# Eight experts on one core: synchronisation by hand in one section in place of a scheduled kernel

## The chip, the core and the metric

The kernel runs on one core of a Trainium2 chip. The metric is the device time of one execution in microseconds (us), as the median of several runs. A profiler also records one execution: every instruction on the five engines (TensorE for matrix products, VectorE, ScalarE, GpSimd and SyncE) and every packet that the core's 16 DMA engines move between the off-chip memory (HBM) and the on-chip one (SBUF). Products are summed up in PSUM, a small memory that VectorE and ScalarE then read. Engines run by themselves; they wait for each other on semaphores, which are counters.

## The reference

Eight experts each apply a layer with a ReLU and a second layer to their own 256 rows. All arrays are float32.

```
n_experts, capacity, hidden, expert_hidden = 8, 256, 512, 2048
h = np.matmul(x, w1) + b1[:, np.newaxis, :]
h = np.maximum(h, 0)
return (np.matmul(h, w2) + b2[:, np.newaxis, :]).astype(np.float32)
```

Here w1 is 8 x 512 x 2048 and w2 is 8 x 2048 x 512: 4.19 MB per expert and array, 67 MB in all. x and the output have 4.19 MB each.

## The kernel before, in words

The kernel is written for a tile framework: buffers come from pools with a number of copies each, and the framework's scheduler puts in all semaphores. `ordered` keeps an instruction in its written order on its engine.

**Loads.** GpSimd's queue carries all weights, because its transfers convert float32 to float16 on the way (`load_w1`, L84; `load_w2`, L93); the wide loads of x for experts 2 to 3 and 4 to 7 go the same way (`load_x`, L76). x of experts 0 and 1 is loaded as float32 by SyncE (L194) and converted by VectorE (L203). There are three buffers for w1 and three for w2, so the load of expert e waits until TensorE has done with expert e - 3. The list `ring` holds the loads in order, each with the step from which it may be issued. Weights of the last two experts' w2 come in two halves (`HALVED`).

**Steps.** The main loop has steps s = 0 to 10. Step s runs the first product of expert s and the second product of expert s - 3 (`LAG`). TensorE therefore always has the first product of a later expert ahead of the second product of an earlier one; steps 8, 9 and 10 hold only the second products of experts 5, 6 and 7.

**First product** (L121): for each of 16 slices j, four matmuls of 256 columns make the transposed slice of h in a PSUM tile `ph` (three copies). ScalarE adds b1, applies the ReLU and writes `hT` (L128). The right-hand side `xT` comes from VectorE's transposes of 32 x 32 blocks (L109 and L112), which are written in the middle of the first product before.

**Second product** (L171 and L178): for each of the two blocks of 128 rows (tb 0 and 1) one matmul with a row of ones puts in b2, and 16 matmuls of 512 columns add up the slices in PSUM tiles `po`. There are two copies of the pair `po0`, `po1`. For the halved experts the order is: first half of the slices for tb 0 and tb 1, then the second half for both. For the others all 16 of tb 0 come first.

**Store**: VectorE copies `po0` (L156), ScalarE copies `po1` (L157). Results of experts 0 to 3 and of 4 and 5 are collected and written by GpSimd's queue at its end, behind all loads (`flush`, L140). Expert 6 is written in three parts, two by SyncE and one by ScalarE, and expert 7 by SyncE (L164). L252 is the program's own start, L263 its end.

Of the kernel before, what the change touches and what calls it, by code (L numbers as in the profile page):

```python
# [10 lines left out]
def kernel(  # L11
# [8 lines left out]
):  # L20
    nc = tc.nc
    fp32 = mybir.dt.float32
    fp16 = mybir.dt.float16
    E, T, H = x.shape
# [4 lines left out]
    nJ = M // P  # L29
    B = 32  # L30
    nB = P // B
    LAG = 3

    GROUPS = {0: 4, 4: 2}
    HALVED = (E - 2, E - 1)


    PARTS = {E - 2: ((0, 25, False), (25, 121, True), (121, 128, False))}  # L40
    nXF32 = 2
    X_LOADS = {2: 2, 4: 4}

    def ordered(ins):
        return tc.keep_in_program_order(ins)

    singles = ctx.enter_context(tc.tile_pool(name="singles", bufs=1))
    w1_pool = ctx.enter_context(tc.tile_pool(name="w1", bufs=3))
    w2_pool = ctx.enter_context(tc.tile_pool(name="w2", bufs=3))
    x_pool = ctx.enter_context(tc.tile_pool(name="xp", bufs=1))  # L50
    xT_pool = ctx.enter_context(tc.tile_pool(name="xTp", bufs=2))
    hT_pool = ctx.enter_context(tc.tile_pool(name="hT", bufs=LAG + 1))
    group_pool = ctx.enter_context(tc.tile_pool(name="groups", bufs=1))
    out_pool = ctx.enter_context(tc.tile_pool(name="outp", bufs=2))
# [3 lines left out]
    ones1 = singles.tile([1, P], fp16)  # L58
    b2_sb = singles.tile([1, E * H], fp16)
    b1_rows = singles.tile([E * nB, M // nB], fp32)  # L60
    b1T = singles.tile([P, nJ * B + nB - 1], fp32)

    x16 = [None] * E
    xT = [None] * E
    w1_sb = [None] * E
    w2_sb = [None] * E
    hT = [None] * E
    pending = {}
    results = {}
    group_of = {first + i: (first, n) for first, n in GROUPS.items() for i in range(n)}  # L70

    def load_x(first, n):

        R = n * T // P
        t = x_pool.tile([P, R, H], fp16, tag=f"x{first}", name=f"x{first}")
        ordered(nc.gpsimd.dma_start(  # L76
            out=t, in_=x[first : first + n].rearrange("e (p r) h -> (e p) r h", r=R)
        ))
        for i in range(n):
            x16[first + i] = (t, i * (P // n), R)  # L80

    def load_w1(e):
        w1_sb[e] = w1_pool.tile([P, nKC, M], fp16, tag="w1", name="w1sb")
        ordered(nc.gpsimd.dma_start(  # L84
            out=w1_sb[e], in_=w1[e].rearrange("(p kc) m -> p kc m", kc=nKC)
        ))

    def load_w2(e):
        src = w2[e].rearrange("(p j) h -> p j h", j=nJ)
        w2_sb[e] = w2_pool.tile([P, nJ, H], fp16, tag="w2", name="w2sb")  # L90
        half = nJ // 2 if e in HALVED else nJ
        for lo in range(0, nJ, half):
            ordered(nc.gpsimd.dma_start(out=w2_sb[e][:, lo : lo + half], in_=src[:, lo : lo + half]))  # L93

    def transposes(e):


        t, p0, R = x16[e]
        n = R // nTB
        xT[e] = xT_pool.tile([P, nKC, T], fp16, tag="xT", name="xT")  # L100
        for g in range(T // R // B):
            src = t[p0 + B * g : p0 + B * (g + 1)]
            for b in range(nB):
                block = src[:, :, b * (H // nB) : (b + 1) * (H // nB)].rearrange(
                    "p (n tb) (i kc) -> p tb kc n i", tb=nTB, kc=nKC)
                out = xT[e][b * B : (b + 1) * B].rearrange(
                    "p kc (tb g i n) -> p tb g kc n i", tb=nTB, i=B, n=n)
                if n == 1:
                    nc.vector.transpose(out=out[:, :, g, :, 0, :], in_=block[:, :, :, 0, :])  # L109
                    continue  # L110
                for tb in range(nTB):
                    nc.vector.transpose(out=out[:, tb, g], in_=block[:, tb])  # L112

    def first_product(e):
        hT[e] = hT_pool.tile([P, nJ, T], fp16, tag="hT", name="hT")
        split = group_of[e][1] if e in group_of else 1
        for j in range(nJ):
            bias_at = j * B + e * nB + nB - 1
            ph = psum_h.tile([P, T], fp32, tag="ph", name="ph")
            for kc in range(nKC):  # L120
                ordered(nc.tensor.matmul(  # L121
                    out=ph,
                    lhsT=w1_sb[e][:, kc, :].rearrange("p (q j) -> p q j", j=nJ)[:, :, j],
                    rhs=xT[e][:, kc, :],
                    start=(kc == 0),
                    stop=(kc == nKC - 1),
                ))
            nc.scalar.activation(  # L128
                out=hT[e][:, j, :].rearrange("p (tb k i) -> p tb k i", tb=nTB, k=split),
                in_=ph.rearrange("p (tb i k) -> p tb k i", tb=nTB, k=split),  # L130
                func=mybir.ActivationFunctionType.Relu,
                bias=b1T[:, bias_at : bias_at + 1],
                scale=1.0,
            )
            if j == nJ // 2 and e + 1 < E:
                transposes(e + 1)

    def flush(first):
        dst, src = pending.pop(first)
        ordered(nc.gpsimd.dma_start(out=dst, in_=src))  # L140

    def store(e, po):
        if e in group_of:
            first, n = group_of[e]
            split, rows = n, P // n
            if e == first:
                results[e] = group_pool.tile(
                    [P, split * nTB, H], fp32, tag=f"out{e}", name=f"out{e}")
        else:
            first, n, split, rows = e, 1, 1, P  # L150
            results[e] = out_pool.tile([P, nTB, H], fp32, tag="out", name="out")
        out_sb = results[first]
        at = (e - first) * rows
        for k in range(split):
            part = slice(k * rows, (k + 1) * rows)
            nc.vector.tensor_copy(out=out_sb[at : at + rows, k * nTB, :], in_=po[0][part])  # L156
            nc.scalar.copy(out=out_sb[at : at + rows, k * nTB + 1, :], in_=po[1][part])  # L157
        dst = out[first : first + n].rearrange("e (p r) h -> (e p) r h", r=split * nTB)
        if e in group_of:
            if e == first + n - 1:  # L160
                pending[first] = (dst, out_sb)
            return
        for p0, p1, scalar in PARTS.get(e, ((0, P, False),)):
            (nc.scalar if scalar else nc.sync).dma_start(out=dst[p0:p1], in_=out_sb[p0:p1])  # L164

    def second_product(e):
        po = []
        for tb in range(nTB):
            t = psum_o.tile([P, H], fp32, tag=f"po{tb}", name=f"po{tb}")
            po.append(t)  # L170
            ordered(nc.tensor.matmul(  # L171
                out=t, lhsT=ones1, rhs=b2_sb[0:1, e * H : (e + 1) * H], start=True, stop=False,
            ))
        half = nJ // 2 if e in HALVED else nJ
        for lo in range(0, nJ, half):
            for tb in range(nTB):
                for j in range(lo, lo + half):
                    ordered(nc.tensor.matmul(  # L178
                        out=po[tb],
                        lhsT=hT[e][:, j, tb * P : (tb + 1) * P],  # L180
                        rhs=w2_sb[e][:, j, :],
                        start=False,
                        stop=(j == nJ - 1),
                    ))
        store(e, po)

    warm = singles.tile([1, P], fp16)
    nc.vector.memset(ones1, 1.0)  # L188
    ordered(nc.scalar.activation(out=warm, in_=ones1, func=mybir.ActivationFunctionType.Relu))  # L189
    ordered(nc.scalar.dma_start(out=b1_rows, in_=b1.rearrange("e (b i) -> (e b) i", b=nB)))  # L190
    x32 = []
    for e in range(nXF32):
        x32.append(out_pool.tile([P, nTB, H], fp32, tag="out", name="x32"))
        nc.sync.dma_start(out=x32[e], in_=x[e].rearrange("(p tb) h -> p tb h", tb=nTB))  # L194
    load_w1(0)
    ordered(nc.gpsimd.dma_start(  # L196
        out=b2_sb,
        in_=b2.rearrange("e h -> (e h)").rearrange("(o f) -> o f", o=1),
    ))

    for e in range(nXF32):
# [3 lines left out]
        if e == 0:  # L205
            transposes(e)
# [22 lines left out]
    for s in range(E + LAG):  # L229
# [3 lines left out]
        if s < E:  # L233
            first_product(s)
# [33 lines left out]
```

## Time and profile before

| | |
|---|---|
| time, median of 3 runs | 181.53 us (181.39 to 182.13) |
| span of the profiled execution, first to last instruction | 179.7 us |
| median less span | 1.8 us |
| mean granted TensorE clock | 0.919 |
| transfers on GpSimd's queue | 38.28 MB, 96.4% of the 16 engines' time |

The profiled execution has no time of its own beside its span; 1.8 us is what the median of the runs has over it. A page of the profile gives the busy time of each engine, the span cut into 40 slices with one digit each (9 is 90% busy or more), the DMA queues, the chain of work that ended last, and groups of instructions by line. PE is TensorE, PEld its loading of the stationary operand, DVE is VectorE, ACT ScalarE, POOL GpSimd and SP SyncE; a q behind an engine means its instruction queue. In a row such as `158.43 1.17 ACT L157 COPY ... [10.26 <-PE po L178]` the numbers are the start and the length in us, and the bracket tells how long the engine had been idle and what ended that. In the waits view a row reads: who waited, for whom, us in total, times, longest. A group's row gives busy us, mean ns of one, and the idle time ahead of it with its cause.

### The profile page before, as it was taken

Reading aid. Unit: us, or ns where it says so; the run is one execution under the profiler, and the core shown is the slowest. Engines: PE = TensorE matmul, PEld = TensorE weight load, DVE = VectorE, ACT = ScalarE, POOL = GpSimd, SP = SyncE. Lnnn points to the kernel's source line nnn. Section 1 sums busy time; section 2 is a strip of 40 time slices with the busy share of each in tenths; the row PEclk is TensorE's granted clock in tenths of the full one; section 3 lists DMA queues with packets and bytes.
Section 4 is the critical chain, followed back from the end, with each engine's and each line's share of the span. In section 5 each row is a group of like instructions: output and inputs, shape, how many; then the busy total and the mean of one; then the engine's idle time right before and its main releaser. Section 6 shows DMA issues by size and latency. Waiting matters only on the chain.

```text
span 179.7 us, 1958 instructions
## 1 busy us (share of the span) xinstructions
PE 130.7 (73%) x784; PEld 87.4 (49%) x784; DVE 87.4 (49%) x125; ACT 71.0 (40%) x152; POOL 12.5 (7%) x27
## 2 busy tenths in 40 slices
PE   0005999159895970999769994959499986999960
PEld 0004899149793320794359543934189432434420
DVE  0999938990000199999998699203200020301010
ACT  3001699318793022491267406930559020020010
POOL 6000030200201010001100001000200021010000
PEclk9999999858999696599988999999969997899998
DMA  5999999999998999999999999999999999999995
GB/s 208 274 197 213 233 204 208 230 224 193 228 233 184 224 233 219 193 230 230 193 219 233 212 197 233 230 193 219 233 208 201 233 212 202 217 215 213 344 422 239
DMA packets 3844, 40.56 MB, mean 226 GB/s; under 512 B 460, under 2 KB 476, under 8 KB 1148
## 3 DMA queue, kind: packets, MB, share of 16 engines
q0 software_dynamic: 3200, 38.28, 96.4%
q1 hardware_dynamic: 476, 1.70, 2.5%
q10 hardware_dynamic: 160, 0.46, 0.6%
q8 instruction: 6, 0.10, 0.2%
q14 instruction: 2, 0.02, 0.0%
HBM read 71.39 MB, written 4.19 MB: 421 GB/s over the span
## 4 chain that ended last, share of the span: by engine, by line
DMA 67%; PE 27%; POOL 1%; issue 1%; ACT 0%; another core or an unknown queue 0%; POOLq 0%
DMA w1sb<-in_w_dram 44%; DMA w2sb<-in_w_dram 23%; PE po L178 17%; PE ph L121 10%; PE po L171 1%; POOL w1sb L84 1%; ACT out L157 0%; POOL b_sb L196 0%; POOL x L76 0%; POOLq L252 0%
## 5 line engine op out<-in xcount | busy, mean ns | idle before, releaser
L121 PE MATMUL ph<-xT,w1sb 128*128 128x256 f16 x512 | 66.7, 299 | 36.2 <-DMA w1sb<-in_w_dram 30.0
L121 PEld LDWEIGHTS <-w1sb 128*128 128x128 f16 x512 | 60.9, 148 | 42.7 <-DMA w1sb<-in_w_dram 38.6
L128 ACT ACTIVATE hT<-ph,b1T 128x256 f16<-128x256 f32 x128 | 56.7, 475 | 36.9 <-PE ph L121 22.1
L112 DVE STREAM_TRANSPOSE xT<-x 32x256 f16<-32x256 f16 (+1 forms) x64 | 52.7, 885 | 28.0 <-DMA x<-in_x_dram 22.0
L178 PE MATMUL po<-w2sb,hT 128*128 128x512 f16 x256 | 59.9, 395 | 6.6 <-DMA w2sb<-in_w_dram 6.5
L178 PEld LDWEIGHTS <-hT 128*128 128x128 f16 x256 | 25.7, 101 | 40.7 <-issue 14.4
L156 DVE COPY out<-po 32x512 f32<-32x512 f32 (+2 forms) x22 | 15.1, 688 | 52.5 <-PE po L178 52.2
L157 ACT COPY out<-po 32x512 f32<-32x512 f32 (+2 forms) x22 | 12.7, 578 | 65.5 <-PE po L178 65.3
L109 DVE STREAM_TRANSPOSE xT<-x 32x256 f16<-32x256 f16 x32 | 14.0, 436 | 0.5
L93 POOL DMA_DIRECT2D w2sb<-in_w_dram x10 | 5.3, 535 | 73.9 <-PE po L178 73.9
L84 POOL DMA_DIRECT2D w1sb<-in_w_dram x8 | 4.5, 559 | 62.7 <-PE ph L121 61.9
L171 PE MATMUL po<-b_sb,ones 1*128 1x512 f16 x16 | 4.8, 379 | 0.0
L210 DVE STREAM_TRANSPOSE b1T<-b_rows 32x512 f32<-32x512 f32 x4 | 4.1, 1028 | 0.0
L203 DVE CAST x<-x 128x1024 f16<-128x1024 f32 x2 | 1.4, 694 | 3.3 <-DMA x<-in_x_dram 3.3
L171 PEld LDWEIGHTS <-ones 1*128 1x128 f16 x16 | 0.9, 92 | 2.1 <-issue 2.1
L140 POOL DMA_DIRECT2D out_dram<-out x2 | 1.1, 540 | 11.1 <-ACT out L157 11.1
L189 ACT ACT_TABLE_LOAD x1 | 1.3, 1283 | 0.7 <-PEq L252 0.7
L76 POOL DMA_DIRECT2D x<-in_x_dram x2 | 1.1, 557 | 0.0
L188 DVE MEMSET ones<- 1x128 f16 x1 | 0.2, 165 | 0.8 <-PEq L252 0.8
L196 POOL DMA_DIRECT2D b_sb<-in_b_dram x1 | 0.5, 507 | 0.0
L189 ACT ACTIVATE warm<-ones 1x128 f16<-1x128 f16 x1 | 0.3, 308 | 0.0
L252 POOL MEMSET const-float32-0.0<- 128x1 f32 x1 | 0.1, 98 | 0.2 <-issue 0.2
(3 smaller groups left out, 0.3 us busy)
## 6 DMA issues: line engine op xcount, KB each, us to landing
w1sb<-in_w_dram POOLq DMA_DIRECT2D x8, 2048.0 KB, 37.0
w2sb<-in_w_dram POOLq DMA_DIRECT2D x6, 2048.0 KB, 49.7
w2sb<-in_w_dram POOLq DMA_DIRECT2D x4, 1024.0 KB, 24.0
out_dram<-out POOLq DMA_DIRECT2D x1, 2048.0 KB, 26.7
x<-in_x_dram SPq DMA_DIRECT2D x2, 512.0 KB, 4.0
x<-in_x_dram POOLq DMA_DIRECT2D x1, 1024.0 KB, 35.6
out_dram<-out POOLq DMA_DIRECT2D x1, 1024.0 KB, 17.7
x<-in_x_dram POOLq DMA_DIRECT2D x1, 512.0 KB, 24.5
```

The costliest lines, as they stand in the source:

```text
L84: ordered(nc.gpsimd.dma_start(out=w1_sb[e], in_=w1[e].rearrange("(p kc) m -> p kc m", kc=nKC)))
L93: ordered(nc.gpsimd.dma_start(out=w2_sb[e][:, lo : lo + half], in_=src[:, lo : lo + half]))
L109: nc.vector.transpose(out=out[:, :, g, :, 0, :], in_=block[:, :, :, 0, :])
L112: nc.vector.transpose(out=out[:, tb, g], in_=block[:, tb])
L121: ordered(nc.tensor.matmul(out=ph, lhsT=w1_sb[e][:, kc, :].rearrange("p (q j) -> p q j", j=nJ)[:, :, j], rhs=xT[e][:, kc, :], start=(kc == 0),
L128: nc.scalar.activation(out=hT[e][:, j, :].rearrange("p (tb k i) -> p tb k i", tb=nTB, k=split), in_=ph.rearrange("p (tb i k) -> p tb k i", ...
L156: nc.vector.tensor_copy(out=out_sb[at : at + rows, k * nTB, :], in_=po[0][part])
L157: nc.scalar.copy(out=out_sb[at : at + rows, k * nTB + 1, :], in_=po[1][part])
L171: ordered(nc.tensor.matmul(out=t, lhsT=ones1, rhs=b2_sb[0:1, e * H : (e + 1) * H], start=True, stop=False,))
L178: ordered(nc.tensor.matmul(out=po[tb], lhsT=hT[e][:, j, tb * P : (tb + 1) * P], rhs=w2_sb[e][:, j, :], start=False, stop=(j == nJ - 1),))
L189: ordered(nc.scalar.activation(out=warm, in_=ones1, func=mybir.ActivationFunctionType.Relu))
L210: nc.vector.transpose(out=b1T[b * B : (b + 1) * B, nB - 1 - b : nB - 1 - b + nJ * B], in_=b1_rows.rearrange("r (i j) -> r j i", j=nJ),)
```

## The change

The whole body is put into one section (`tc.tile_critical()`) that the scheduler treats as one piece. Within it every buffer is allocated by hand and every wait is written out on a semaphore of the kernel's own. Buffers keep their count (three of w1 and of w2, two of xT, four of hT), with these differences:

- `ph` has four PSUM buffers, not three; TensorE takes two credits at a time, one per buffer, and ScalarE gives one back with each activation.
- `po` has one pair, not two. TensorE takes `s_free[tb]` before it starts tb of the next expert; VectorE (tb 0) or ScalarE (tb 1) gives it after the copy.
- SyncE waits for each landing of weights and then counts up `s_go`; TensorE takes counts from that one semaphore and doesn't wait for a transfer itself.
- All experts' second products run in two halves of the slices, and the bias matmul of tb stands right ahead of the first half of tb.
- Every engine's program is written out one after the other: SyncE's stores of expert 6 stand between the two counts for expert 7's w2.
- At the section's end SyncE waits for all transfers of the output.

The order of the loads on GpSimd's queue, the sizes of all transfers and the number and shapes of the matmuls, activations, transposes and copies are unchanged. The core of the diff:

```diff
-    psum_h = ctx.enter_context(tc.tile_pool(name="psum_h", bufs=3, space=bass.MemoryType.PSUM))
-    psum_o = ctx.enter_context(tc.tile_pool(name="psum_o", bufs=2, space=bass.MemoryType.PSUM))
+    ctx.enter_context(tc.tile_critical())
+    ph = ctx.enter_context(nc.psum_tensor("ph", [P, NPH, H], fp32))
+    po = ctx.enter_context(nc.psum_tensor("po", [P, nTB, H], fp32))
+    def load(engine, key, **kw):
+        landed[key] = sem(f"d_{key}")
+        engine.dma_start(**kw).then_inc(landed[key], 16)
...
     def load_w1(e):
+        if e >= NW:
+            nc.gpsimd.wait_ge(s_ph, nJ * (e - NW + 1))
...
     def load_w2(e):
+        if e >= NW:
+            nc.gpsimd.wait_ge(s_po[1], e - NW + 1)
...
+    def flush(first):
+        n = GROUPS[first]
+        for tb in range(nTB):
+            nc.gpsimd.wait_ge(s_out[tb], first + n)
...
+    def evict(e, tb):
...
+        engine.wait_ge(s_po[tb], e + 1)
+        for k in range(n):
+            last = copy(out=results[e][at : at + rows, k * nTB + tb, :],
+                        in_=po[k * rows : (k + 1) * rows, tb, :])
+        last.then_inc(s_out[tb], 1)
+        if e + 1 < E:
+            engine.wait_ge(s_out[tb], e + 1)
+            engine.sem_inc(s_free[tb], 1)
...
+    def go(key, n=1):
+        nc.sync.wait_ge(landed[key], 16)
+        nc.sync.sem_inc(s_go, n)
     for s in range(E + LAG):
+        if s == 0:
+            nc.sync.wait_ge(landed["b2"], 16)
         if s < E:
+            go(f"w1_{s}")
+        e = s - LAG
+        if e >= 0 and e not in HALVED:
+            go(f"w2_{e}_0", 2)
+        elif e == E - 2:
+            go(f"w2_{e}_0")
+            go(f"w2_{e}_{half}")
+        elif e == E - 1:
+            go(f"w2_{e}_0")
+            for tb in range(nTB):
+                nc.sync.wait_ge(s_out[tb], e)
+            store(E - 2, 0, 25, nc.sync)
+            store(E - 2, 121, P, nc.sync)
+            go(f"w2_{e}_{half}")
+    for tb in range(nTB):
+        nc.sync.wait_ge(s_out[tb], E)
+    store(E - 1, 0, P, nc.sync)
...
+    def take(s, n=1):
+        nc.tensor.wait_ge(s, n).then_inc(s, -n)
+    for s in range(E + LAG):
+        nc.tensor.wait_ge(s_credit, NPH)
+        if s < E:
+            take(s_go)
+            take(s_xT)
+            for j in range(nJ):
+                if j % 2 == 0:
+                    take(s_credit, 2)
+                for kc in range(nKC):
+                    last = nc.tensor.matmul(
...
+                last.then_inc(s_ph, 1)
         if s >= LAG:
+            for lo in range(0, nJ, half):
+                take(s_go)
+                for tb in range(nTB):
+                    if lo == 0:
+                        take(s_free[tb])
+                        nc.tensor.matmul(po[:, tb, :], ones1[:], b2_sb[:, e * H : (e + 1) * H],
+                                         start=True, stop=False)
+                    for j in range(lo, lo + half):
+                        last = nc.tensor.matmul(
...
+                    if lo:
+                        last.then_inc(s_po[tb], 1)
+    for key, done in landed.items():
+        if key.startswith("out"):
+            nc.sync.wait_ge(done, 16)
```

More of the change, by code (lines that the diff above doesn't have):

```diff
@@ L23 @@
     fp16 = mybir.dt.float16
+    relu = mybir.ActivationFunctionType.Relu
     E, T, H = x.shape
@@ L29 @@
     nJ = M // P
+    half = nJ // 2
     B = 32
@@ L59 @@
[L59 to L68, printed above, removed]
-    results = {}
-    group_of = {first + i: (first, n) for first, n in GROUPS.items() for i in range(n)}
-    def load_x(first, n):
-        R = n * T // P
[L75 to L80, printed above, removed]
@@ L82, in load_w1, with sbuf, sem @@
-    def load_w1(e):
[L83 to L86, printed above, removed]
+    group_of = {first + i: (first, n) for first, n in GROUPS.items() for i in range(n)}
+    ctx.enter_context(tc.tile_critical())
+    def sbuf(name, shape, dtype):
+        return ctx.enter_context(nc.sbuf_tensor(name, shape, dtype))
+    def sem(name):
+        return ctx.enter_context(nc.semaphore(name=name))
@@ new lines @@
+    ones1 = sbuf("ones1", [1, P], fp16)
+    warm = sbuf("warm", [1, P], fp16)
+    b2_sb = sbuf("b2_sb", [1, E * H], fp16)
+    b1_rows = sbuf("b1_rows", [E * nB, M // nB], fp32)
+    b1T = sbuf("b1T", [P, nJ * B + nB - 1], fp32)
+    w1_sb = sbuf("w1_sb", [P, NW * nKC * M], fp16)
+    w2_sb = sbuf("w2_sb", [P, NW * nJ * H], fp16)
+    xT = sbuf("xT", [P, 2 * nKC * T], fp16)
+    hT = sbuf("hT", [P, (LAG + 1) * nJ * T], fp16)
+    x32 = [sbuf(f"x32_{e}", [P, nTB, H], fp32) for e in range(2)]
+    x16 = {}
@@ new lines @@
+    for e in range(2):
+        x16[e] = (sbuf(f"x_{e}", [P, nTB, H], fp16), 0, nTB)
+    x_group = {}
+    for first, n in X_LOADS.items():
+        R = n * T // P
+        x_group[first] = sbuf(f"x_{first}", [P, R, H], fp16)
+        for i in range(n):
+            x16[first + i] = (x_group[first], i * (P // n), R)
+    results = {}
+    for first, n in GROUPS.items():
+        t = sbuf(f"out_{first}", [P, n * nTB, H], fp32)
+        for i in range(n):
+            results[first + i] = t
+    results[E - 2], results[E - 1] = x32
@@ new lines @@
+    ph = ctx.enter_context(nc.psum_tensor("ph", [P, NPH, H], fp32))
+    po = ctx.enter_context(nc.psum_tensor("po", [P, nTB, H], fp32))
+    landed = {}
+    def load(engine, key, **kw):
+        landed[key] = sem(f"d_{key}")
+        engine.dma_start(**kw).then_inc(landed[key], 16)
+    s_ones = sem("ones")
+    s_self = sem("dve_self")
+    s_b1 = sem("b1T")
+    s_xT = sem("xT")
+    s_ph = sem("ph")
+    s_credit = sem("ph_free")
+    s_po = [sem(f"po{tb}") for tb in range(nTB)]
+    s_free = [sem(f"po{tb}_free") for tb in range(nTB)]
@@ new lines, with load_x @@
+    s_out = [sem(f"out{tb}") for tb in range(nTB)]
+    s_go = sem("weights")
+    for e in range(2):
+        load(nc.sync, f"x{e}", out=x32[e][:], in_=x[e].rearrange("(p tb) h -> p tb h", tb=nTB))
+    def load_x(first):
+        n = X_LOADS[first]
+        R = n * T // P
+        load(nc.gpsimd, f"x{first}", out=x_group[first][:],
+             in_=x[first : first + n].rearrange("e (p r) h -> (e p) r h", r=R))
+    def load_w1(e):
+        if e >= NW:
+            nc.gpsimd.wait_ge(s_ph, nJ * (e - NW + 1))
+        at = e % NW * nKC * M
+        load(nc.gpsimd, f"w1_{e}",
+             out=w1_sb[:, at : at + nKC * M].rearrange("p (kc m) -> p kc m", kc=nKC),
+             in_=w1[e].rearrange("(p kc) m -> p kc m", kc=nKC))
@@ L88, in load_w2 @@
     def load_w2(e):
+        if e >= NW:
+            nc.gpsimd.wait_ge(s_po[1], e - NW + 1)
+        dst = w2_sb[:, e % NW * nJ * H : (e % NW + 1) * nJ * H].rearrange("p (j h) -> p j h", j=nJ)
         src = w2[e].rearrange("(p j) h -> p j h", j=nJ)
[L90 to L93, printed above, removed]
+        size = half if e in HALVED else nJ
@@ new lines, in load_w2 @@
+        for lo in range(0, nJ, size):
+            load(nc.gpsimd, f"w2_{e}_{lo}", out=dst[:, lo : lo + size], in_=src[:, lo : lo + size])
+    def flush(first):
+        n = GROUPS[first]
+        for tb in range(nTB):
+            nc.gpsimd.wait_ge(s_out[tb], first + n)
+        load(nc.gpsimd, f"out{first}", in_=results[first][:],
+             out=out[first : first + n].rearrange("e (p r) h -> (e p) r h", r=n * nTB))
+    load_w1(0)
+    load(nc.gpsimd, "b2", out=b2_sb[:],
+         in_=b2.rearrange("e h -> (e h)").rearrange("(o f) -> o f", o=1))
@@ new lines @@
+    for s in range(1, E + LAG - 1):
+        if s < E:
+            if s in X_LOADS:
+                load_x(s)
+            load_w1(s)
+        if s >= LAG:
+            load_w2(s - LAG)
+    load_w2(E - 1)
+    for first in GROUPS:
+        flush(first)
+    nc.vector.memset(ones1[:], 1.0).then_inc(s_ones, 1)
+    nc.scalar.wait_ge(s_ones, 1)
+    nc.scalar.activation(out=warm[:], in_=ones1[:], func=relu)
+    load(nc.scalar, "b1", out=b1_rows[:], in_=b1.rearrange("e (b i) -> (e b) i", b=nB))
@@ L99, in transposes @@
         n = R // nTB
-        xT[e] = xT_pool.tile([P, nKC, T], fp16, tag="xT", name="xT")
+        if e >= 2:
+            first = max(f for f in X_LOADS if f <= e)
+            nc.vector.wait_ge(landed[f"x{first}"], 16)
+            nc.vector.wait_ge(s_ph, nJ * (e - 1))
+        mine = xT[:, e % 2 * nKC * T : (e % 2 + 1) * nKC * T].rearrange("p (kc t) -> p kc t", kc=nKC)
+        last = None
         for g in range(T // R // B):
@@ L111, in transposes @@
                 for tb in range(nTB):
[L112 to L152, printed above, removed]
-        at = (e - first) * rows
[L154 to L199, printed above, removed]
@@ L201 @@
-    for e in range(nXF32):
-        t = x_pool.tile([P, nTB, H], fp16, tag=f"x{e}", name=f"x{e}")
-        nc.vector.tensor_copy(out=t, in_=x32[e])
-        x16[e] = (t, 0, nTB)
+                    last = nc.vector.transpose(out=dst[:, tb, g], in_=block[:, tb])
+        last.then_inc(s_xT, 1)
+    def evict(e, tb):
+        engine = nc.scalar if tb else nc.vector
+        copy = nc.scalar.copy if tb else nc.vector.tensor_copy
+        first, n = group_of.get(e, (e, 1))
+        rows = P // n
+        at = (e - first) * rows
+        engine.wait_ge(s_po[tb], e + 1)
[6 more added lines that the diff above has]
+            engine.sem_inc(s_free[tb], 1)
@@ L205, with store @@
+    def store(e, p0, p1, engine):
+        dst = out[e].rearrange("(p r) h -> p r h", r=nTB)
+        load(engine, f"out{e}_{p0}", out=dst[p0:p1], in_=results[e][p0:p1])
+    for e in range(2):
+        nc.vector.wait_ge(landed[f"x{e}"], 16)
+        nc.vector.tensor_copy(out=x16[e][0][:], in_=x32[e][:]).then_inc(s_self, 1)
+        nc.vector.wait_ge(s_self, e + 1)
         if e == 0:
             transposes(e)
+    nc.vector.wait_ge(landed["b1"], 16)
     for b in range(nB):
-        nc.vector.transpose(
+        last = nc.vector.transpose(
@@ L225 @@
-    ring.append((E + LAG - 3, load_w2, (E - 1,)))
-    for first, n in GROUPS.items():
-        ring.append((first + n + LAG, flush, (first,)))
+    last.then_inc(s_b1, 1)
+    for s in range(E + LAG):
+        if s + 1 < E:
+            transposes(s + 1)
+        if s >= LAG:
+            evict(s - LAG, 0)
+    nc.scalar.wait_ge(s_b1, 1)
+    for s in range(E + LAG):
+        if s < E:
+            split = group_of.get(s, (s, 1))[1]
+            if s > LAG:
+                nc.scalar.wait_ge(s_po[1], s - LAG)
+            for j in range(nJ):
+                at = (s % (LAG + 1) * nJ + j) * T
+                bias_at = j * B + s * nB + nB - 1
+                nc.scalar.wait_ge(s_ph, nJ * s + j + 1)
+                nc.scalar.activation(
+                    out=hT[:, at : at + T].rearrange("p (tb k i) -> p tb k i", tb=nTB, k=split),
+                    in_=ph[:, j % NPH, 0:T].rearrange("p (tb i k) -> p tb k i", tb=nTB, k=split),
+                    func=relu,
+                    bias=b1T[:, bias_at : bias_at + 1],
+                    scale=1.0,
+                ).then_inc(s_credit, 1)
+        if s >= LAG:
+            evict(s - LAG, 1)
+        if s - LAG == E - 2:
+            for tb in range(nTB):
+                nc.scalar.wait_ge(s_out[tb], E - 1)
+            store(E - 2, 25, 121, nc.scalar)
```

59 lines of the change are left out of this document (31 added, 28 removed).

## The prediction

> **What bounds the kernel now.** I read the page's slices and queues first, since they say whether an engine or the transfers set the pace.
>
> ```profile
> span 179.7 us, 1958 instructions
> PE 130.7 (73%) x784; PEld 87.4 (49%) x784; DVE 87.4 (49%) x125; ACT 71.0 (40%) x152; POOL 12.5 (7%) x27
> DMA  5999999999998999999999999999999999999995
> q0 software_dynamic: 3200, 38.28, 96.4%
> HBM read 71.39 MB, written 4.19 MB: 421 GB/s over the span
> ```
>
> The DMA row stands at 9 in all but three of the 40 slices, and GpSimd's queue alone fills 96.4% of the sixteen engines' time, while TensorE is busy 73%. So transfers set the pace, and only their start, their end and a gap in them can move the time. The windows view shows how full the stretches are (columns: stretch and its length, busy time of five engines, granted clock, DMA share, GB/s).
>
> ```profile
> 0.70:1.90 1.20, 0.00 (x0) 0.00 (x0) 0.17 (x1) 1.16 (x1) 0.65 (x1) 1.00 0.18 27
> 15.40:60.00 44.60, 36.04 (x267) 31.40 (x268) 21.15 (x50) 28.29 (x64) 4.26 (x8) 0.91 1.01 215
> 60.00:120.00 60.00, 46.77 (x286) 31.89 (x285) 48.29 (x44) 28.18 (x60) 2.11 (x4) 0.90 1.01 216
> 120.00:169.20 49.20, 43.64 (x213) 22.37 (x213) 6.20 (x9) 12.35 (x25) 3.17 (x6) 0.93 1.02 222
> 173.50:175.20 1.70, 0.00 (x0) 0.00 (x0) 0.00 (x0) 0.59 (x1) 0.00 (x0) 1.00 1.05 436
> 175.20:176.50 1.30, 0.00 (x0) 0.00 (x0) 0.00 (x0) 0.00 (x0) 0.00 (x0) 1.00 0.99 416
> 176.50:177.60 1.10, 0.00 (x0) 0.00 (x0) 0.00 (x0) 0.00 (x0) 0.00 (x0) 1.00 0.83 343
> 177.60:178.80 1.20, 0.00 (x0) 0.00 (x0) 0.00 (x0) 0.00 (x0) 0.00 (x0) 0.69 0.34 137
> 178.80:179.70 0.90, 0.00 (x0) 0.00 (x0) 0.00 (x0) 0.00 (x0) 0.00 (x0) 0.50 0.00 0
> ```
>
> A share of about 1 from 15.4 to 176.5 us: the stream never pauses. The last 0.9 us carry no transfer; that is the program's end. Does TensorE also have a part? The chain of waits from 108 us on says so:
>
> ```profile
> 108.47 41.12 DMA w2sb<-in_w_dram
> 149.59 0.04 issue
> 149.63 8.75 PE po L178 x32
> 158.39 0.53 PE po L171 x2
> 158.92 7.01 PE po L178 x32
> 165.93 0.53 PE po L171 x2
> 166.47 7.03 PE po L178 x32
> 173.49 0.02 issue
> 173.52 0.59 ACT out L157
> ```
>
> From 149.6 on TensorE runs without a break: the second products of experts 5, 6 and 7. But the transfers keep up with it to the end. Two tile views, each cut to one or two DMAs, tell when they land:
>
> ```profile
> L93 POOL DMA_DIRECT2D w2sb<-in_w_dram x2: 527/531/535, 147.3 to 147.8; - x2
> DMA to landing us min/median/max: 16.9/19.1/21.4
> ```
>
> ```profile
> L164 SPq DMA_DIRECT2D out_dram<-out x1: 361/361/361, 174.1 to 174.1; - x1
> DMA to landing us min/median/max: 4.7/4.7/4.7
> ```
>
> The halves of expert 7's w2 land at 147.3 + 16.9 = 164.2 and 147.8 + 21.4 = 169.2. TensorE wants the second half sixteen matmuls into the last product, at about 166.5 + 3.5 = 170.0, so it is 0.8 us behind the stream. The last store goes out at 174.1 and lands at 178.8. The end has two near-equal limits, the queue of transfers and TensorE's last 24 us.
>
> **The change part by part.**
>
> The stream in the middle: nothing, 0.0. GpSimd issues the same loads in the same order, and waits for the same events (the last reader of the buffer three experts back), now as counters. The wait that would hurt is one that lets the queue run dry.
>
> ```profile
> POOL w2sb L93 <- PE po L178: 73.9, 5, 18.9
> L121 PE MATMUL ph<-xT,w1sb 128*128 128x256 f16 x512 | 66.7, 299 | 36.2 <-DMA w1sb<-in_w_dram 30.0
> L128 ACT ACTIVATE hT<-ph,b1T 128x256 f16<-128x256 f32 x128 | 56.7, 475 | 36.9 <-PE ph L121 22.1
> ```
>
> GpSimd's longest wait is 18.9 us, yet the last load was issued at 147.3 with expert 5's w2 landing at 149.6 and all of expert 6's still to come: two loads took 169.2 - 149.6 = 19.6 us, so 2.3 + 9.8 = 12 us of work lay ahead. A counter seen a few tenths late is hidden. The first product takes its PSUM credits by twos from four buffers; it may fall to ScalarE's pace, 16 x 0.475 = 7.6 us per expert, against the 66.7 / 8 = 8.3 us that it takes at its mean. That is hidden by the 36.2 us in which it waits mostly for w1. Without that cover half a microsecond per expert would still be far under the 12 us. Halving the order of experts 0 to 5 costs nothing there for the same reason.
>
> The section's entry: one synchronisation of the engines may be added before the first load; and at its exit, before the program's own end, one drain and join. Nothing in this trace is such a section; the nearest rows are the program's own start (L252) and end (L263).
>
> ```profile
> SPq L252 <- PEq L252: 0.7, 1, 0.7
> SPq L263 <- PEq L263: 0.7, 2, 0.5
> ```
>
> Bounds for the entry: 0 and 0.7 (a whole second start); it cannot gain, because the loads already leave right behind the start. I take 0.15, near a bare join, as the engines have nothing to drain. Everything later shifts by it. For the exit: two joins at the end cost 0.7 together, so one costs 0.2 to 0.5. I take 0.25; ends -0.4 (the section's own waits make part of the old ending's 0.9 us short) and +0.7.
>
> The end, TensorE's side. SyncE now waits for each landing and passes on a count. Before, the release took 0.04 us ("issue" at 149.59). A row for two queues in series is missing; I take 0.2, so +0.15. In sequence behind SyncE's waits stand later counts and three stores, and only TensorE waits for the counts. The two bias matmuls of expert 5 were done before the landing; now they stand behind the count.
>
> ```profile
> 146.89 0.60 PE L171 MATMUL po<-b_sb,ones 1*128 1x512 f16 x2
> 154.97 1.39 DVE L156 COPY out<-po 64x512 f32<-64x512 f32 x2 [10.04 <-PE po L178]
> 158.43 1.17 ACT L157 COPY out<-po 64x512 f32<-64x512 f32 x2 [10.26 <-PE po L178]
> 164.24 0.69 DVE L156 COPY out<-po 128x512 f32<-128x512 f32 x1 [7.88 <-PE po L178]
> 165.97 0.59 ACT L157 COPY out<-po 128x512 f32<-128x512 f32 x1 [6.38 <-PE po L178]
> ```
>
> They began at 146.89, before 149.59; the chain prices such a pair at 0.53, so +0.53. Next, one PSUM pair: expert 6 must find po 0 evicted. Expert 5 now ends at 149.8 + 8.75 + 0.53 = 159.1; in halves, po 0 is complete eight matmuls earlier (8 x 7.01 / 32 = 1.75), at 157.3. VectorE's two copies take 1.39, to 158.7, and two hops to free it reach 158.9 to 159.3: a stall of 0 to 0.2, I take 0.1. po 1 is needed 0.27 + 1.75 = 2.0 us into expert 6, and ScalarE's 1.17 fit in. For expert 7 both copies are short (0.69 in 1.75, 0.59 in 2.0), no stall. SyncE sends two stores of expert 6 ahead of the last count: evicted at about 166.7 + 0.7 = 167.4, two issues of some 0.45 (the two x loads take 0.87, quoted below), done by 168.3, before the landing at 169.2. If that cover failed, the last product would stall for what is missing.
>
> TensorE's end is therefore 0.15 + 0.53 + 0.1 = 0.8 late, and the last store is issued at 174.9. Does that move the end? The traffic after 175.2 is 416 x 1.3 + 343 x 1.1 + 137 x 1.2 = 1082 KB, of which the last store is 524 KB; the other 558 KB would keep the engines busy alone for 1.3 us, until 176.5. From issue to first bytes I estimate 1.0 us, from the start of the timeline:
>
> ```profile
> 0.74 0.87 SPq L194 DMA_DIRECT2D x<-in_x_dram  x2
> ```
>
> The first x load is issued at 0.74, and a share of 0.18 in 0.7 to 1.9 means 0.2 us busy, from about 1.7. Issued at 174.9, the store begins at 175.9, while the others still fill the engines. So up to 175.5 - 174.1 = 1.4 us of delay is covered, and 0.8 costs little: I take +0.1, bounds 0 and 0.8.
>
> The Trainium skill, in "Advanced Engine Details and Errata", section "Network/Comms", puts a sequencer's reading of a semaphore at 50 to 100 ns. By that the hop through SyncE would cost about 0.1 (an estimate) in place of 0.15, and the end would stay covered; no row of this trace shows the hop.
>
> Standalone waits on TensorE. The end's list shows how far its sequencer runs ahead:
>
> ```profile
> L263 PEldq DRAIN  x2: 13/2044/4075, 169.5 to 179.3; - x2
> L263 PEldq EVENT_SEMAPHORE  x2: 51/51/51, 179.1 to 179.7; - x2
> ```
>
> It reached the final drain at 169.5 and waited 4.1 us for the matmuls, so waits of 0.051 each, already satisfied, pass in that lead: 0. If none were hidden, the 15 or so behind 149.6 would cost 15 x 0.051 = 0.8.
>
> **The sum.** Entry 0.15, stream 0, end 0.1, exit 0.25: +0.5 on the profiled span, 180.2. The span is 179.7 and the median of the runs 181.53; the 1.8 between them lie outside and I leave them. So 181.53 + 0.5 = 182.0.
>
> **The rivals.** *The PSUM pair becomes the bound, slower.* If evictions are not covered in the run of the last three products, TensorE waits for whole copies: 1.39 before expert 6 and 0.69 before expert 7, with four hops of 0.2, 2.9 more; with the 0.7 for bias and hop, 3.6 late less the 1.4 covered gives 2.2, and with the boundaries 0.4 a time of 184.1. It decides only beyond 1.4 us of delay; half of those waits gives 182.7. For it: the copies and the quarter product that hides them differ by only 0.36. Against: two of three experts have a margin of 1 us.
>
> The Trainium skill speaks for this rival: "Perfetto Trace Analysis", section "Matmul Optimizations", wants all PSUM banks leveraged for parallelism, and the change cuts the second product's buffers by half. The trace agrees only where TensorE is not waiting for loads, the last 24 us.
>
> *Boundaries at full price, slower:* 0.7 + 0.7 + 0.1 = 1.5, 183.0; for it, the start and end each cost that here. *Nothing moves:* the boundaries are nearly free and the tail is covered, 181.5; the change replaces counters with counters. *Faster:* the ending shrinks and the last transfers draw closer together: of 177.6 to 178.8 only a third is used, and the 0.9 behind it could lose 0.4; 0.5 + 0.4 gives 180.6. Against: a faster TensorE can't bring it, as the loads end at 169.2 and 4.19 MB of output at 416 to 436 GB/s take 9.6 to 10.1 us more, to 178.8 at the earliest.
>
> **How the numbers follow.** Forecast, 181.7 to 182.4: 0.44. Nothing moves: 0.20. PSUM pair: 0.17, half of it above 183.2. Boundaries: 0.13. Faster: 0.06. About 0.5% (0.9 us) is what a measurement of this kernel can tell from no change. Within it lie the first two but for 0.01 of the forecast, 0.63; slower 0.31; faster 0.06. The range 181.1 to 183.2 leaves out the faster case and the upper half of the PSUM rival, 0.15, and some of the extreme bounds.
>
> **What would show it.** The DMA row still at 9 throughout, and w2's last landing at 169.2 plus the entry's shift. In the waits view, TensorE stalls on po 0 at expert 6 by no more than 0.2. The last product ends about 0.8 later, and the last landing only 0.1 later beyond the shift. Start and end stretches longer by 0.15 and 0.25. A gap in the stream, a first load leaving over a microsecond late, or copies on the chain between the last products would prove me wrong.

## The result, and the profile after

The changed kernel takes 184.06 us, median of 4 runs (183.78 to 184.81), against 181.47 before: slower, ratio 1.0141, 95% interval 1.0112 to 1.0169. The prediction was 182.0, the range 181.1 to 183.2. The profiled execution of the changed kernel has a span of 182.0 us and a time of 183.78.

The page of the changed kernel first: the span, the DMA share by slices, and GpSimd's queue.

```profile
span 182.0 us, 2100 instructions
DMA  5999998999999999999999999999999899999991
q0 software_dynamic: 3200, 38.28, 95.2%
```

The queue's packets are as many as before, and the share stands at 8 or more everywhere but in the first and the last slice; the last fell from 5 to 1. That points to the end. The windows view of the changed kernel, with the columns as above:

```profile
0.95:1.90 0.95, 0.00 (x0) 0.00 (x0) 0.17 (x1) 0.95 (x1) 0.44 (x1) 1.00 0.00 0
15.40:60.00 44.60, 33.95 (x265) 30.40 (x265) 21.51 (x50) 28.33 (x64) 4.24 (x8) 0.92 1.01 215
120.00:169.40 49.40, 43.97 (x217) 21.44 (x218) 7.12 (x10) 12.07 (x25) 3.18 (x6) 0.97 1.02 221
176.50:177.60 1.10, 0.00 (x0) 0.00 (x0) 0.00 (x0) 0.00 (x0) 0.00 (x0) 0.50 0.89 369
177.60:178.95 1.35, 0.00 (x0) 0.00 (x0) 0.00 (x0) 0.00 (x0) 0.00 (x0) 0.50 0.42 170
178.95:181.97 3.02, 0.00 (x0) 0.00 (x0) 0.00 (x0) 0.00 (x0) 0.00 (x0) 0.50 0.00 0
```

From 15.4 to 169.4 the DMA share and the rate are those of before, and no slice up to the last shows a pause. Then, behind the last landing, the stretch without any transfer is 3.02 us long, where it was 0.90: 2.1 of the 2.3 us by which the span grew. Two tile views of the changed kernel, cut to the last halves of w2 and to the last store, give the landings:

```profile
L86 POOL DMA_DIRECT2D w_sb<-in_w_dram x2: 530/534/537, 148.4 to 149.0; - x2
DMA to landing us min/median/max: 15.9/18.2/20.5
```

```profile
L86 SPq DMA_DIRECT2D out_dram<-x x1: 361/361/361, 174.1 to 174.1; - x1
DMA to landing us min/median/max: 4.9/4.9/4.9
```

The last weights land at 149.0 + 20.5 = 169.5 and the last store at 179.0, 0.3 and 0.2 later than before. That is about the later start: the first load of x leaves at 0.95, not at 0.74.

```profile
0.95 0.87 SPq L86 DMA_DIRECT2D x<-in_x_dram  x2
```

What fills the 3.02 us stands in the list of the section's own instructions (L44) in the changed kernel. A drain is the instruction at which an engine waits for its own work: TensorE's at the end of the kernel before stood from 169.5 until the last matmul was through at 173.5. The list's columns are queue, operation and count, durations in ns (least, median, most), and first and last start. Beneath it is SyncE's row of the waits view.

```profile
L44 SPq COMPARE_BRANCH  x1: 32/32/32, 179.0 to 179.0; - x1
L44 ACTq DRAIN  x1: 8/8/8, 179.2 to 179.2; - x1
L44 POOLq DRAIN  x1: 1929/1929/1929, 179.2 to 179.2; - x1
L44 DVEq DRAIN  x1: 17/17/17, 179.2 to 179.2; - x1
L44 PEldq DRAIN  x1: 8/8/8, 179.2 to 179.2; - x1
L44 SPq DRAIN  x1: 7/7/7, 179.3 to 179.3; - x1
```

```profile
SPq L44 <- POOLq L44: 1.7, 1, 1.7
```

SyncE leaves the section at 179.0, behind its wait for the last store. Only then, at 179.2 and 179.3, do the engines begin their drains. Four of them need 7 to 17 ns, GpSimd's needs 1929, and SyncE waits 1.7 us for it. Now GpSimd's row in the list of the program's end (L263) of the kernel before:

```profile
L263 POOLq DRAIN  x3: 45/101/18684, 159.9 to 179.4; - x3
```

GpSimd drained there as well, and for 18.7 us, but from 159.9 on, straight behind the issue of its last transfer. It was through at 159.9 + 18.7 = 178.6, ahead of the last landing at 178.8.

The Trainium skill, in "VectorE: DVE Perf Modes", section "The DRAIN you can't avoid", calls the drains ahead of and behind a kernel boilerplate of about 12 ns, constant on all five engines. The section's drains agree with that for four engines (7 to 17 ns) but not for GpSimd (1929 ns). The page doesn't speak of a section's exit; GpSimd's drain at the program's own end, 18684 ns here and 1929 in no_pool_drain below, isn't of that length either. The measurement decides.

### The profile page after: what moved, and what is told of

Its sections match the earlier page's. It is cut to its first block, busy times and chain, and to the rows that moved or that the text cites. A ratio compares the mean times of both kernels' runs of the same rounds, so it can differ in the third digit from the quotient of the medians.

```text
span 182.0 us, 2100 instructions
## 1 busy us (share of the span) xinstructions
PE 126.8 (70%) x784; PEld 84.2 (46%) x784; DVE 87.6 (48%) x125; ACT 70.6 (39%) x152; POOL 12.5 (7%) x27
## 5 line engine op out<-in xcount | busy, mean ns | idle before, releaser
L287 PE MATMUL ph<-xT,w_sb 128*128 128x256 f16 x512 | 62.8, 287 | 36.7 <-PEq L273 36.7
L287 PEld LDWEIGHTS ph<-xT,w_sb 128*128 128x128 f16 x512 | 58.7, 147 | 41.6 <-issue 39.4
L307 PE MATMUL po<-w_sb,hT 128*128 128x512 f16 x256 | 59.6, 387 | 0.0
L307 PEld LDWEIGHTS po<-w_sb,hT 128*128 128x128 f16 x256 | 24.1, 99 | 31.2 <-issue 5.5
L185 DVE COPY out<-po 32x512 f32<-32x512 f32 (+1 forms) x20 | 13.7, 687 | 40.3 <-PE po L307 40.1
L185 ACT COPY out<-po 32x512 f32<-32x512 f32 (+1 forms) x20 | 11.6, 578 | 55.0 <-PE po L307 54.8
L86 POOL DMA_DIRECT2D w_sb<-in_w_dram x18 | 9.7, 544 | 137.8 <-PE po L307 72.9
L303 PE MATMUL po<-b_sb,ones 1*128 1x512 f16 x16 | 6.2, 385 | 9.9 <-PEq L273 9.9
L303 PEld LDWEIGHTS po<-b_sb,ones 1*128 1x128 f16 x16 | 1.4, 90 | 15.9 <-issue 15.9
L185 DVE COPY x<-po 128x512 f32<-128x512 f32 x2 | 1.4, 692 | 13.4 <-PE po L307 13.4
## 6 DMA issues: line engine op xcount, KB each, us to landing
out_dram<-out POOLq DMA_DIRECT2D x1, 1024.0 KB, 18.1
```

Source lines behind the costliest of these rows:

```text
L86: engine.dma_start(**kw).then_inc(landed[key], 16)
L185: last = copy(out=results[e][at : at + rows, k * nTB + tb, :], in_=po[k * rows : (k + 1) * rows, tb, :])
L287: last = nc.tensor.matmul(ph[:, j % NPH, 0:T], w1_sb[:, w_from : w_from + (P - 1) * nJ + 1 : nJ], xT[:, x_at + kc * T : x_at + (kc + 1) * ...
L303: nc.tensor.matmul(po[:, tb, :], ones1[:], b2_sb[:, e * H : (e + 1) * H], start=True, stop=False)
L307: last = nc.tensor.matmul(po[:, tb, :], hT[:, h_from : h_from + P], w2_sb[:, w_at + j * H : w_at + (j + 1) * H], start=False, stop=(j == n ...
```

## The experiments

**Theory "drain":** GpSimd's drain settles the transfers that it issued, which takes 1.9 us here; the section puts the drain's start behind the last landing, so nothing hides it. **Rival "tail":** the PSUM pair, SyncE's counts or the moved bias matmuls delay the last products. **Rival "section":** the price lies in the section's exit as such.

### early_drain

```diff
     for first in GROUPS:
         flush(first)
+    nc.gpsimd.drain()
```

> The changed kernel, with one drain more on GpSimd, right behind its last transfer of the output (issued at 159.7 us in the changed kernel's trace). Theory 'drain': the 1.93 us at the section's exit are GpSimd's drain, which settles its transfers and starts only when the section ends at 179.2; begun earlier it runs beside the last transfers, ends at about 178.7 as in the kernel before, and the drain at the exit shrinks to below 0.1. Time 184.1 - 1.9 = 182.2. Rival 'fixed price': every drain of GpSimd in a section costs 1.9 wherever it stands; then the exit still has 1.9 and the time stays at 184.1. Rival 'tail': the loss lies in the last products, so 184.1 as well, with the exit unchanged.

Measured: 182.22 us (182.18 to 182.53), ratio to before 1.0034, interval 1.0021 to 1.0046. From this kernel's lists, the new drain (L147) and the exit's, and below them its windows view:

```profile
L147 POOLq DRAIN  x1: 19071/19071/19071, 159.8 to 159.8; - x1
```

```profile
L44 POOLq DRAIN  x1: 47/47/47, 179.4 to 179.4; - x1
```

```profile
177.60:179.15 1.55, 0.00 (x0) 0.00 (x0) 0.00 (x0) 0.00 (x0) 0.00 (x0) 0.75 0.38 156
179.15:180.48 1.33, 0.00 (x0) 0.00 (x0) 0.00 (x0) 0.00 (x0) 0.00 (x0) 0.50 0.00 0
```

One instruction more takes back 1.8 us: the drain runs from 159.8 to 178.9 beside the last transfers, the one at the exit shrinks to 0.047, and the silent end from 3.02 to 1.33. That refutes "fixed price" and leaves at most 0.6 us (182.22 against 181.61) for "tail" and everything else.

### no_pool_drain

```diff
-    ctx.enter_context(tc.tile_critical())
+    ctx.enter_context(tc.tile_critical(no_gpsimd_drain=True))
```

> The changed kernel with the section told to leave out GpSimd's drain at its exit; all else as it is. Theory 'drain': what GpSimd has to settle is only moved; the program's own end drains GpSimd too, and that drain, 0.04 us in the changed kernel, now takes about 1.9. Time within 0.3 of 184.1. If the drain at the exit is a wait that nothing needs, 182.2. The two answers tell whether the price belongs to the section or to the first drain after the last transfer.

Measured: 183.90 us (183.79 to 184.01), ratio 1.0121, interval 1.0106 to 1.0136. The list of the program's end (L345) in this kernel:

```profile
L345 POOLq DRAIN  x3: 45/69/1929, 179.6 to 181.9; - x3
```

The same 1929 ns came a step later, at 179.6 in the program's own end, as the first answer had it. The price doesn't belong to the section's exit but to the first drain behind GpSimd's transfers.

### late_drain

```diff
     assert not ring and not pending
+    ordered(nc.gpsimd.memset(results[E - 1][:, 0, 0:1], 0.0))
```

The added write clears a column of the on-chip copy that has been stored already.

> The kernel before with one instruction more: at its very end GpSimd writes one column of expert 7's result buffer, and so has to wait until the last store has read it. No section, no hand-made wait, no other change. Its drain at the program's end can then start only behind the last landing at 178.8, as in the changed kernel, and not at 159.9. Theory 'drain': the drain takes 1.93 behind that landing, nothing hides it, and the time is 181.5 + 1.9 + 0.2 for the write = 183.6. Rival 'section': the price comes with the section's own exit; then the drain stays short and the time is at most 181.8.

Measured: 183.55 us (183.51 to 183.86), ratio 1.0111, interval 1.0097 to 1.0126. The list of the program's end (L264) in this kernel:

```profile
L264 POOLq DRAIN  x3: 45/107/2064, 178.9 to 181.5; - x3
```

The kernel before, with no section and no hand-made wait, loses 1.9 us (183.55 against 181.61) as soon as GpSimd has to wait for the last landing. Its drain takes 2.06 us behind it, in which the added write of 0.10 us falls. With early_drain this shows the cause from both sides. In the changed kernel it is SyncE's written wait for the stores, inside the section, that comes ahead of the drains; no run leaves that wait out.

### halved_w1

```diff
-        load(nc.gpsimd, f"w1_{e}",
-             out=w1_sb[:, at : at + nKC * M].rearrange("p (kc m) -> p kc m", kc=nKC),
-             in_=w1[e].rearrange("(p kc) m -> p kc m", kc=nKC))
+        dst = w1_sb[:, at : at + nKC * M].rearrange("p (kc m) -> p kc m", kc=nKC)
+        src = w1[e].rearrange("(p kc) m -> p kc m", kc=nKC)
+        for lo in range(0, nKC, 2):
+            load(nc.gpsimd, f"w1_{e}_{lo}", out=dst[:, lo : lo + 2], in_=src[:, lo : lo + 2])
```

SyncE waits for both halves before it counts.

> The changed kernel with each load of w1 as two transfers of half the size (31 transfers on GpSimd's queue, not 23; same bytes). It asks what sets the 1.93 us of the drain. If GpSimd settles transfer by transfer, 1.93 x 31 / 23 = 2.6; if the price is per packet or fixed, 1.93 again. The time moves by that difference, 184.1 or 184.7.

Measured: 184.76 us in one run. GpSimd's row in the section's list of this kernel, and the row of GpSimd's queue:

```profile
L44 POOLq DRAIN  x1: 2582/2582/2582, 179.6 to 179.6; - x1
```

```profile
q0 software_dynamic: 4352, 38.28, 95.5%
```

That is the expected 2.6 for 31 transfers in place of 23, with the same bytes: neither a fixed price nor one by bytes. But the edit doesn't tell transfers from packets, as the expectation had it. The queue's packets rose as well, from 3200 to 4352, by 1.36, and the transfers by 31 / 23 = 1.35; 1.93 times either gives 2.6. By transfers it comes to 0.653 / 8 = 0.082 us for each, and 23 x 0.082 = 1.88 leaves 0.05, near what a drain with nothing to settle took (0.047); by packets 0.12 would be left. One run of this kind speaks for transfers but doesn't decide it.

### two_pairs

```diff
-    po = ctx.enter_context(nc.psum_tensor("po", [P, nTB, H], fp32))
+    po = ctx.enter_context(nc.psum_tensor("po", [P, 2 * nTB, H], fp32))
...
-        if e + 1 < E:
+        if e + 2 < E:
             engine.wait_ge(s_out[tb], e + 1)
...
-        nc.tensor.sem_inc(s_free[tb], 1)
+        nc.tensor.sem_inc(s_free[tb], 2)
```

and `po[:, e % 2 * nTB + tb, :]` wherever `po[:, tb, :]` stood.

> The changed kernel with two pairs of PSUM buffers for the second product, as before; one part of the change undone. Theory 'drain' says 184.1 with at most 0.2 less, since no wait for a copy is on the chain of the changed kernel's last three products (pieces 7.9, 7.4 and 7.8 us without a gap). Rival 'PSUM pair': the copies hold back TensorE, and the time falls by 1 us or more, to 183.0.

Measured: 183.98 us (183.72 to 184.00), ratio 1.0122, interval 1.0107 to 1.0137, which overlaps that of the changed kernel. The PSUM pair costs nothing that can be measured. In the changed kernel's chain the last three products follow each other without a gap, 7.8 us each (150.07, 157.88 and 165.63 to 173.40).

### tail_undone

```diff
+    nc.gpsimd.drain()
...
+            for tb in range(nTB):
+                take(s_free[tb])
+                nc.tensor.matmul(po[:, e % 2 * nTB + tb, :], ones1[:], b2_sb[:, e * H : (e + 1) * H],
+                                 start=True, stop=False)
             for lo in range(0, nJ, half):
-                take(s_go)
+                if lo == 0 or e in HALVED:
+                    nc.tensor.wait_ge(landed[f"w2_{e}_{lo}"], 16)
                 for tb in range(nTB):
-                    if lo == 0:
-                        take(s_free[tb])
-                        nc.tensor.matmul(po[:, tb, :], ones1[:], b2_sb[:, e * H : (e + 1) * H],
-                                         start=True, stop=False)
```

with the two pairs of two_pairs, a like wait for w1, and SyncE left with its stores. The order in halves stays.

> The changed kernel with the early drain and with the other parts of the change undone: two pairs of PSUM buffers, the bias matmuls ahead of the wait for weights, and TensorE waiting for landings itself instead of for SyncE's count. What is left is the section and its hand-made order. The prediction's terms for the tail say that TensorE's last product ends up to 0.8 earlier and the time falls by 0.1 against 182.2 of the early drain, 182.1; rival 'tail': 0.5 or more less, 181.7 or below.

Measured: 182.46 us (182.07 to 182.72), ratio 1.0044, interval 1.0032 to 1.0056, against 1.0021 to 1.0046 of early_drain: no gain. Windows view of tail_undone:

```profile
150.00:153.40 3.40, 3.19 (x8) 1.17 (x9) 0.00 (x0) 0.00 (x0) 0.00 (x0) 0.54 1.04 217
```

The rival asked for 181.7 or below, and the fastest of the six runs took 182.07: undoing the counts by SyncE and the moved bias matmuls brings no time back. What they cost TensorE can't be read from this trace. Here the granted clock was 0.54 during expert 5's first matmuls, and the 32 took 8.77 us in place of 7.12, more than the bias matmuls ahead of the landing saved: the last product ended at 174.1, against 173.6 in early_drain.

### section_on_before, a miss

```diff
     assert not ring and not pending
+    with tc.tile_critical():
+        with nc.sbuf_tensor("mark", [1, P], fp16) as mark:
+            nc.vector.memset(mark[:], 0.0)
```

> The kernel before, with one empty section put behind all its work (a single write of 128 halves by VectorE inside it, on a buffer that nothing reads). It brings the exit alone: no hand-made waits, no PSUM pair fewer, no counts by SyncE. Theory 'drain': if the section's end waits for the last store before it drains GpSimd, the span grows by 1.9 for the drain and 0.3 for the section's joins, 183.7; if GpSimd's drain can start earlier, the growth is only 0.3 or so. Rival 'tail' (PSUM pair, counts): no more than 0.5 in either case, 181.5 to 182.0, and no drain of GpSimd of about 1.9 at the end.

Measured: 184.67 us (184.09 to 185.81), ratio 1.0171, interval 1.0131 to 1.0210. The time is 1.0 us above the 183.7 that the theory expected, and for another reason. The timeline of this kernel shows where the section went, and the waits and windows views what followed:

```profile
15.81 0.11 DVE L240 MEMSET mark<- 1x64 uint32 x1 [14.82 <-DMA w1sb<-in_w_dram]
16.11 0.69 DVE L203 CAST x<-x 128x1024 f16<-128x1024 f32 x1 [0.18 <-DVEq L238]
```

```profile
POOL w1sb L84 <- PE ph L121: 65.8, 5, 33.0
```

```profile
36.00:40.00 4.00, 4.00 (x39) 4.00 (x38) 3.26 (x9) 4.00 (x10) 1.59 (x3) 1.00 0.49 68
```

The scheduler put the section on VectorE ahead of the first conversion of x, where it waited for loads until 15.8. That held up TensorE, w1's fourth load could be issued only after 33.0 us of waiting, and the stream ran half empty from 36 to 40. GpSimd's long drain at the program's end ran hidden as before, for 19.1 us from 162.3 on. So the run says nothing on the exit. It does show that the stream's cover has an end: VectorE's first conversion came at 16.11 and not at 4.24, w1's fourth load left at 37.02 and not at 25.60, and expert 5's w2 landed 2.7 us later (152.27 against 149.59).

### split_store

```diff
+        if e == E - 1:
+            for tb in range(nTB):
+                nc.sync.dma_start(out=dst[:, tb, :], in_=out_sb[:, tb, :])
+            return
```

> The kernel before with the last store, expert 7's 512 KB, sent in two: the rows of po 0 as soon as VectorE has copied them (172.5) and those of po 1 behind ScalarE's copy (174.1). No drain of GpSimd is touched. If the end is set by the transfers alone, all bytes still have to move and the time stays within 0.2 of 181.6. If the last store's latency counts, because the engines are only a third used from 177.6 to 178.8, half the bytes behind the last copy make the last landing 0.4 to 0.6 earlier: 181.1.

Measured: 181.54 us (181.48 to 181.92), ratio 0.9996, interval 0.9984 to 1.0008: no change. The tile view of the two stores in this kernel:

```profile
L165 SPq DMA_DIRECT2D out_dram<-out x2: 360/472/584, 172.3 to 173.9; - x2
DMA to landing us min/median/max: 4.9/5.4/5.9
```

The second, with half the bytes and sent at 173.9, still took 4.9 us (the least of the two) and landed at 178.8, as the whole store did: the end is set by the queued transfers, not by the last copy. No version found here beats the kernel before.

## Why the prediction was wrong, point by point

**The step that failed is the section's exit:** "I take 0.25; ends -0.4 ... and +0.7." It measured 3.02 - 0.90 = +2.1, outside both ends. The prediction named "one drain and join" there and priced the joins alone; GpSimd's drain stood in the sum at nothing, and it took 1.93. The bound was taken from SyncE's waits at the old program's end. Those had been short because GpSimd had drained already. The row that shows the hidden drain, 18684 ns from 159.9, stood in the same list as the two rows that were quoted for TensorE's sequencer, and the prediction doesn't mention it. Its own question, what an edit costs if its cover is gone, wasn't asked of that row. There was a hint of the size: the drain had ended 1.0 us behind GpSimd's last landing (159.9 + 17.7 = 177.6, to 178.6). The full 1.9 no row of before showed.

**Right, with sizes.** The stream in the middle: 0.0, the last weights only 0.3 later, most of it the later start. The entry: 0.15 predicted, 0.21 measured (0.74 to 0.95). The exit's joins without the drain: 3.02 - 0.90 - 1.93 = 0.19 in the changed kernel and 1.33 - 0.90 = 0.43 in early_drain, both inside the bounds that were given, on either side of the 0.25 taken. So the rest of the change, section included, comes to +0.6 in early_drain (182.22 against 181.61), near the +0.5 forecast: the sum lacked one term.

**The tail.** The chain of the changed kernel, from the landing of expert 5's w2 on, and the landing itself from the tile view of that load:

```profile
L86 POOL DMA_DIRECT2D w_sb<-in_w_dram x1: 530/530/530, 109.7 to 109.7; - x1
DMA to landing us min/median/max: 40.1/40.1/40.1
```

```profile
150.03 0.04 issue
150.07 0.37 PE po L303
150.44 1.83 PE po L307 x8
152.27 0.32 PE po L303
152.59 5.29 PE po L307 x24
157.88 0.32 PE po L303
158.19 1.83 PE po L307 x8
...
173.42 0.59 ACT x L185
```

The load landed at 149.8 and TensorE began at 150.07: the hop through SyncE took about 0.3, where 0.2 was taken. The estimate of 0.1 by the Trainium skill ("Advanced Engine Details and Errata", section "Network/Comms") was further off. The bias pair costs 0.37 + 0.32 = 0.69 there, not 0.53. Between the experts there is no gap: the PSUM pair never stalls, as the margins had it. Still TensorE ends 0.1 earlier than before and not 0.8 later, because the 32 matmuls of expert 5 took 1.83 + 5.29 = 7.12 and not 8.75. The windows view tells why, first a row of the kernel before and then two of the changed kernel:

```profile
149.60:153.00 3.40, 3.37 (x11) 1.32 (x11) 0.00 (x0) 0.00 (x0) 0.00 (x0) 0.67 1.04 217
```

```profile
121.40:124.90 3.50, 3.50 (x10) 1.11 (x9) 0.00 (x0) 0.00 (x0) 0.00 (x0) 0.54 1.05 225
150.00:153.40 3.40, 3.33 (x15) 1.29 (x16) 0.00 (x0) 0.00 (x0) 0.02 (x1) 1.00 1.03 214
```

The granted clock stayed at 1.00, where it was 0.67 before. The changed kernel had its dip earlier, at 121.4, where TensorE still waits for loads behind it; early_drain had one at 140.8, where eight matmuls took 3.58 us and not 1.90. So the forecast of the tail, 0.8 later, came out at 0.1 earlier by luck: with the 8.75 of before, TensorE's end would have been about 1.5 late (an estimate, 8.75 - 7.12 - 0.1), near the 1.4 that the prediction held covered. How far that cover reaches, no run tests. The four runs, with spans of 182.0 to 183.0, rank with the mean granted clock, 0.936 down to 0.918. That a dip in the tail makes the longer ones is argued from this and wasn't shown.

**The rivals.** "The PSUM pair becomes the bound" gave 184.1 and 184.06 was measured, but that is chance: two_pairs gives the second pair back and the time stays at 183.98, and none of the last three products waits for a copy, where the prediction thought that it could matter. "Boundaries at full price", 183.0, looked in the right place with the wrong mechanism: the joins cost 0.2 at the entry and 0.2 to 0.4 at the exit, and the drain, which it didn't have, 1.9.

## What to carry to other kernels

In these runs GpSimd's drain grew with the transfers that the engine had issued, and it cost nothing as long as it ran beside other work. What held it back until the last landing, a section's exit or a single late write, exposed it, and a drain right behind GpSimd's last issue gave the time back. Look in the list of the program's end for long instructions that are hidden today, and ask when they'd start after the change. When a kernel's transfers fill the whole span, as here, hand-made waits have nothing to gain inside it; its two ends are left to win or lose, and the middle is lost only if the loads leave later than their cover allows.

## What the hardware showed beyond that

GpSimd's drain cost 0.047 us with nothing to settle, 1.929 after 23 transfers and 2.582 after 31 with the same bytes: about 0.082 for each, if it goes by transfers and not by packets. It cost that though its transfers were done: in the changed kernel the last of them had landed at 159.7 + 18.1 = 177.8, 1.4 us before the drain began. Started early it ended 1.0 us behind the last of GpSimd's landings in the kernel before. On TensorE, two bias matmuls next to each other took 0.53 us, and 0.64 when each stood alone ahead of eight others.
